# One decoder layer on one core: the second norm applied by VectorE, the tile turned in TensorE's transpose mode

## The chip, the core and the metric
The kernel runs on one core of one Trainium2 chip. The metric is the device time of one execution in microseconds (us), here the median of a few runs. A core has five engines that work side by side, each on its own queue in order: TensorE (PE) multiplies matrices and writes to PSUM, VectorE (DVE) and ScalarE (ACT) do elementwise work on SBUF and PSUM, GpSimd (POOL) builds a few constant masks, and SyncE (SP) issues the DMAs.

## What is computed
One layer of a decoder, on 1024 positions of 1024 channels, all float32. The mixer is a multi-scale causal pooling; a gated feed-forward network with a causal convolution follows.

```python
def rms_norm(x, g):
    return x * rsqrt(mean(x * x, axis=-1) + EPS) * g

h = rms_norm(x, norm_mix_g)
# four groups of 256 channels, windows of 2, 4, 8 and 16 positions:
d = causal_window_mean(h) - h
x = x + pool_scale * (einsum('bsgc,gcd->bsgd', d, pool_w) + pool_b)
n = rms_norm(x, norm_ffn_g)                    # the second norm
val, gate = split(causal_conv3(n @ w_in) + b)  # 2 x 2816 channels
x = x + (silu(gate) * val) @ w_out
```

## The kernel before, in words
A tile is 128 positions by 1024 channels, positions on the partitions; there are eight. The work has three parts: the mixer with the second norm (lines 384 to 413), the product with `w_in` for 22 pairs of hidden tiles (lines 263 to 447), and the product with `w_out` (lines 451 to 602). Both large products run as seven products of half-sized blocks (P1 to P7) in place of eight, and each float32 operand is split into a high and a low part in float32r, so that one product becomes three passes on TensorE. ScalarE makes the high part and VectorE subtracts it to get the low part (`split`, lines 67 to 71; `split_n`, lines 257 to 260).

The mixer is a software pipeline. Step j of the loop at line 389 scales the window matrix of tile j by the first norm's factor (`mixer_norm`), forms the windows of tile j-1 on TensorE (`mixer_window`, tile psd, split into dh and dl), multiplies tile j-2 by the pooling weights and adds the residual (`mixer_out`, tile psy), and prepares tile j-4 for the feed-forward part (`ffn_operand`, tile pst). Tiles psd, psy, pst and the edges share three PSUM pairs of banks (`bank2`).

The change is about the second norm. In the kernel before, `mixer_out` (lines 217 to 222) stores the new x1, computes one factor per position from its squares (`rstd_of`), and multiplies a 128x128 identity by that factor: a diagonal. `ffn_operand` (lines 233 to 255) then multiplies each 128x128 block of x1 by the diagonal on TensorE. This turns the block (channels on the partitions) and scales it in one matmul. With the channels on the partitions, the norm's gain is one number per partition: ScalarE applies it to seven blocks as it copies them from PSUM to `n2f` (`ACT_GAIN`, lines 241 to 242), VectorE to the eighth (line 244). The splits and subtractions that feed P1 to P7 then read `n2f`. Tiles 0 to 3 are split into B11 and B21; tiles 4 to 7 are subtracted from them (`sub`, line 271).

The tile framework sets the order on each engine at build time: it goes through the program, issues what its own times say is ready, in program order where several are, and gives out buffers from each pool. Work on an engine then runs strictly in that order. `tc.issue_after` (lines 408 and 421) holds the first splits of `w_in` behind a tile's residual add. The splits of weights, and some x tiles before them, share seven buffers of 4 KB per partition (tag `hl`). Everything in the pool `pre` (constants, the middle x tiles, the window matrices) is given back at line 414, and the later operands T2, T3, B22 and T4 take that room.

Of the kernel before, what the change touches and what calls it, by code (L numbers as in the profile page):

```python
# [7 lines left out]
F32 = mybir.dt.float32  # L8
F32R = mybir.dt.float32r
BF16 = mybir.dt.bfloat16  # L10
AF = mybir.ActivationFunctionType
ALU = mybir.AluOpType
PSUM = bass.MemoryType.PSUM

P = 128
S = 1024
D = 1024
F = 2816
NS = S // P
NK = D // P  # L20
NF = F // P
NG = 4
# [6 lines left out]
GF = GM + NK  # L29
# [1 line left out]

FAC = P
B0 = FAC + 2 * NG * HALO
BD = B0 + NG * P

NOPS_A = 3
ACT_GAIN = 7

NH = 512
NP2 = NF // 2  # L40
# [3 lines left out]
def trunk_kernel(ctx: ExitStack, tc: tile.TileContext, x, consts, par, rows, pool_w, w_in, w_out, out):  # L44
    nc = tc.nc
# [5 lines left out]
    work = ctx.enter_context(tc.tile_pool(name="work", bufs=1))  # L51
# [3 lines left out]
    pp = pre.enter_context(tc.tile_pool(name="pre", bufs=1, side="right"))  # L55
# [18 lines left out]
    xs = {}  # L74

    def load_x(j):
        if j < 2 or j == NS - 1:
            xs[j] = work.tile([P, D], F32, tag="hl", name=f"x{j}", bufs=7)
        else:
            xs[j] = pp.tile([P, D], F32, tag="x", name=f"x{j}", bufs=5)  # L80
        nc.sync.dma_start(xs[j], x[j * P : (j + 1) * P, :])

    cst = pp.tile([P, BD], F32, tag="cst", name="cst")
# [20 lines left out]
    par_sb = const.tile([P, NPAR], F32, tag="par", name="par_sb")  # L104
# [6 lines left out]
    nc.sync.dma_start(par_sb, par)  # L111
    nc.sync.dma_start(scale_b, rows[:1, :].to_broadcast([P, D]))
    load_x(1)
    for g in range(0, NG, 2):
        nc.sync.dma_start(wp_raw[:, 2 * g : 2 * g + 4, :], pool_w[g : g + 2].rearrange("g (k p) d -> p (g k) d", p=P))
    load_x(2)
# [5 lines left out]
    nc.vector.memset(eps_t, EPS)  # L122
    ident = cst[:, :FAC]
    fac = cst[:, FAC:B0].rearrange("p (c t) -> p c t", t=HALO)
    band0 = cst[:, B0:].rearrange("p (g s) -> p g s", s=P)

    def rstd_of(src, name):
        junk = pp.tile([P, D], BF16, tag="junk", name=f"junk_{name}")
# [22 lines left out]
            nc.tensor.matmul(ps[:, c * P : (c + 1) * P], src[:, c * P : (c + 1) * P], weights[:, c // 2, :], start=True, stop=True)  # L151


    bias_hl = pp.tile([P, D], F32R, tag="bias_hl", name="bias_hl")
    mean_w = pp.tile([P, P], F32R, tag="mean_w", name="mean_w")

    def mixer_bias():
        nc.vector.memset(mean_w.bitcast(F32), 2.0 / P)
        nc.vector.tensor_tensor(bias_b, bias_b, scale_b, ALU.mult)
        nc.scalar.activation(bias_hl, bias_b, AF.Copy)  # L160
        low = slice(P // 2, P)
        nc.vector.tensor_tensor(bias_hl[low, :], bias_b[low, :], bias_hl[low, :].bitcast(F32), ALU.subtract)
# [20 lines left out]
                nc.scalar.activation(wph[:, cs, :], wp_raw[:, cs, :], AF.Copy)  # L183
                nc.vector.tensor_tensor(wpl[:, cs, :], wp_raw[:, cs, :], wph[:, cs, :].bitcast(F32), ALU.subtract)

    ds = {}

    def mixer_window(j):
        ps = bank2(f"psd{j}")
# [13 lines left out]
    n2s = {}  # L203
    x1_dram = dram.tile([S, D], F32, tag="x1_dram", name="x1_dram")

    def mixer_out(j):
        dh, dl = ds.pop(j)
        ps = bank2(f"psy{j}")
        for h in range(2):
            cols = slice(h * NH, (h + 1) * NH)  # L210
            for c in range(4 * h, 4 * h + 4):
                o = ps[:, c // 2 * GRP : (c // 2 + 1) * GRP]
                for i, (a, w) in enumerate(((dh, wph), (dh, wpl), (dl, wph))):
                    nc.tensor.matmul(o, a[:, c, :], w[:, c, :], start=c % 4 == 0 and i == 0, stop=False, skip_group_check=True)  # L214
            nc.tensor.matmul(ps[:, cols], mean_w, bias_hl[:, cols], start=False, stop=True, skip_group_check=True)
        x1 = xs.pop(j)
        marks[j] = nc.vector.tensor_tensor(x1, ps, x1, ALU.add).ins
        nc.sync.dma_start(x1_dram[j * P : (j + 1) * P, :], x1)
        r = rstd_of(x1, f"b{j}")
        diag = pp.tile([P, P], F32, tag="diag", name=f"diag{j}", bufs=2)  # L220
        nc.vector.tensor_scalar(diag, ident, r, None, op0=ALU.mult)
        n2s[j] = (x1, diag)

    n2f = n2_pool.tile([P, NK, S], F32, tag="n2f", name="n2f")
    nops = {}
# [5 lines left out]
        nops[b] = nop_tile(nop_a, b)  # L231

    def ffn_operand(j):
        x1, diag = n2s.pop(j)
        ps = bank2(f"pst{j}")
        for c in range(NK):
            nc.tensor.matmul(ps[:, c * P : (c + 1) * P], x1[:, c * P : (c + 1) * P], diag, start=True, stop=True)  # L237
        cols = slice(j * P, (j + 1) * P)
        ps3 = ps.rearrange("p (c s) -> p c s", c=NK)
        gain = par_sb[:, GF : GF + NK]  # L240
        for c in range(ACT_GAIN):
            nc.scalar.activation(n2f[:, c, cols], ps3[:, c, :], AF.Identity, scale=gain[:, c : c + 1])
        rest = slice(ACT_GAIN, NK)
        nc.vector.tensor_tensor(n2f[:, rest, cols], ps3[:, rest, :], gain[:, rest].unsqueeze(2).to_broadcast([P, NK - ACT_GAIN, P]), ALU.mult)
        lo, hi = slice(0, 4), slice(4, 8)
        if j < NS // 2:
            split_n(nops["B11"], n2f[:, lo, cols], cols)
            split_n(nops["B21"], n2f[:, hi, cols], cols)
            return
        cols0 = slice(cols.start - NH, cols.stop - NH)  # L250
        b11, b12, b21, b22 = n2f[:, lo, cols0], n2f[:, lo, cols], n2f[:, hi, cols0], n2f[:, hi, cols]
        sub(b11, b12, b11)
        split_n(nops["T1"], b11, cols0)
        sub(b12, b22, b12)
        sub(b21, b21, b22)

    def split_n(t, src, cols=slice(None), ks=slice(None)):
        h = t[:, 0, ks, cols]
        nc.scalar.activation(h, src, AF.Copy)
        nc.vector.tensor_tensor(t[:, 1, ks, cols], src, h.bitcast(F32), ALU.subtract)  # L260
# [9 lines left out]
    def sub(out, a, b):  # L270
        nc.vector.tensor_tensor(out, a, b, ALU.subtract)  # L271
# [117 lines left out]
    for j in range(NS + 4):  # L389
        if j < NS:  # L390
            mixer_norm(j)
        if j == 0:
            edge_norm()
            stat(1)
        if 0 <= j - 1 < NS:
            mixer_window(j - 1)
        if j == 1:
            mixer_edges()
            mixer_weights()
            mixer_bias()  # L400
        if 0 <= j - 2 < NS:
            mixer_out(j - 2)
        if 0 <= j - 4 < NS:
            ffn_operand(j - 4)
        if j in (4, 6):
            load_in(j // 2 - 2)
        if 5 <= j <= 8:
            with tc.issue_after(marks[j - 2]):
                prep_event(j - 5)
        if j in (8, 10, 11):  # L410
            event((8, 10, 11).index(j))
        stat(j + 2)
        stat(j + 1)
# [10 lines left out]
    lo, hi = slice(0, 4), slice(4, 8)  # L424
    halves = [slice(0, 2), slice(2, 4)]
    t1, t3, b22, t4 = n2f[:, lo, s0], n2f[:, lo, s1], n2f[:, hi, s1], n2f[:, hi, s0]
# [119 lines left out]
    for k in range(-SLOOK, len(oevents)):  # L546
        p, f = oevents[k + SLOOK] if k + SLOOK < len(oevents) else (None, 0)
# [11 lines left out]
        p, f = oevents[k]  # L559
# [45 lines left out]
def constants():  # L605

    import numpy as np

    r, t, h = np.arange(P)[:, None], np.arange(P), np.arange(HALO)
    blocks = [np.eye(P)]  # L610
    blocks += [np.tile(w / np.minimum(h + 1, w), (P, 2)) for w in WINDOWS]
    inside = [(r > t - w) & (r <= t) for w in WINDOWS]
    blocks += [(m - np.eye(P) * np.minimum(t + 1, w)) / w for m, w in zip(inside, WINDOWS)]
    return np.concatenate(blocks, axis=1).astype(np.float32)


# [32 lines left out]
```

## Time and profile before
| | |
|---|---|
| median of 3 runs | 721.17 us (720.72 to 721.32) |
| the profiled execution | 723.45 us |
| its span, first to last instruction | 721.7 us |
| mean granted TensorE clock | 0.995 |
| ScalarE, busy share of the span | 49% |
| HBM read, written | 63.34 MB, 19.92 MB |

In a row of the timeline stand the start, the busy time, the engine, the line and operation, output and inputs, shapes and the count; in brackets, how long the engine idled before and what released it. Consecutive operations on one engine overlap a little in these rows, so what an operation costs its engine is the distance from its start to the next start. In a row of a group stand, after the bar, the busy time and the mean of one in ns, then the idle time ahead. A float32 matmul shows as two starts. A stretch's row begins with its two ends and its length.

### The profile page before, as it was taken

The page shows a single profiled execution, that of the slowest core. Times are in us where ns is not written, and L with a number is a line of the kernel's source. Part 1 is how long each engine was busy: PE and PEld are TensorE (multiplying, and loading weights), DVE is VectorE, ACT ScalarE, POOL GpSimd, SP SyncE. Part 2 cuts the span into 40 slices and gives each one's busy share as a digit, 9 for nine tenths or more (in the row PEclk, how much of TensorE's full clock was granted, in tenths as well). Part 3 has the DMA queues.
Part 4 walks back from the last instruction along what each step waited for, and adds up shares of the span by engine and source line. Part 5 has one row for each costly group of instructions (what it writes and reads, how often), then busy time and mean ns, then how long its engine had stood idle before and what let it go on. Part 6 is the DMA issues. An engine that isn't in the chain of part 4 may idle for free.

```text
span 721.7 us, 8803 instructions
## 1 busy us (share of the span) xinstructions
PE 698.9 (97%) x3252; PEld 580.2 (80%) x3252; DVE 609.7 (84%) x941; ACT 352.3 (49%) x566; POOL 7.7 (1%) x33
## 2 busy tenths in 40 slices
PE   3799999999999999999999999999999999999997
PEld 3799977888888888888888888888888788888886
DVE  3788999999888898888888888877996998798994
ACT  4597746554444444444444444444553444344441
POOL 4000000000000000000000000000000000000000
PEclk9899999999999999999999999999999999999999
DMA  9722030222222222222122112227999910005241
GB/s 266 282 89 84 34 117 0 118 88 88 88 87 88 88 88 89 87 88 81 66 89 73 58 75 87 88 89 264 315 321 312 308 54 1 0 1 190 87 152 67
DMA packets 30881, 83.83 MB, mean 116 GB/s; under 512 B 3335, under 2 KB 4487, under 8 KB 28023
## 3 DMA queue, kind: packets, MB, share of 16 engines
q1 hardware_dynamic: 30839, 83.28, 32.8%
q8 instruction: 25, 0.41, 0.2%
q14 instruction: 17, 0.14, 0.1%
HBM read 63.34 MB, written 19.92 MB: 115 GB/s over the span
## 4 chain that ended last, share of the span: by engine, by line
PE 80%; DVE 11%; DMA 6%; issue 1%; SPq 1%; ACT 1%; DVEq 0%; ACTq 0%
PE Y L303 23%; PE oP L576 21%; PE X L303 15%; PE Z L303 15%; PE psy L214 3%; DMA blk<-g_dram 3%; PE psd L151 2%; DMA x<-in_x_dram 1%; PE pst L237 1%; DVE n2f L271 1%; DVE oBP L70 1%; DVE T L260 1%; DMA blk<-in_w_out_dram 1%; DVE blk L271 1%; DVE oAP L70 1%
## 5 line engine op out<-in xcount | busy, mean ns | idle before, releaser
L576 PE MATMUL oP<-oBP,oAP 128*128 128x512 f32 x924 | 210.8, 390 | 1.0 <-ACT oBP L69 0.6
L576 PEld LDWEIGHTS oP<-oBP,oAP 128*128 128x128 f32 x924 | 173.2, 188 | 38.5 <-DVE oBP L70 1.4
L303 PE MATMUL X<-B,A11s 128*128 128x512 f32 x264 | 65.6, 394 | 0.7 <-DVE A11s L70 0.7
L303 PE MATMUL Y<-T,S2s 128*128 128x512 f32 x264 | 65.1, 394 | 1.1 <-DVE T L260 1.0
L303 PE MATMUL Z<-B,S4s 128*128 128x512 f32 x264 | 64.1, 392 | 0.6 <-DVE r L337 0.6
L303 PE MATMUL Z<-T,S1s 128*128 128x512 f32 x264 | 64.6, 393 | 0.0
L303 PE MATMUL Y<-T,S3s 128*128 128x512 f32 x264 | 64.3, 392 | 0.0
L303 PE MATMUL Y<-T,A22s 128*128 128x512 f32 x264 | 64.1, 392 | 0.0
L303 PE MATMUL X<-B,A12s 128*128 128x512 f32 x264 | 63.4, 390 | 0.0
L303 PEld LDWEIGHTS Y<-T,S2s 128*128 128x128 f32 x264 | 49.2, 188 | 13.2 <-DVE T L260 1.5
L303 PEld LDWEIGHTS X<-B,A11s 128*128 128x128 f32 x264 | 49.3, 188 | 12.3 <-DVE A11s L70 1.1
L303 PEld LDWEIGHTS Z<-B,S4s 128*128 128x128 f32 x264 | 49.5, 188 | 11.8 <-issue 1.1
L303 PEld LDWEIGHTS Z<-T,S1s 128*128 128x128 f32 x264 | 49.5, 188 | 11.4 <-ACT S1s L69 0.2
L303 PEld LDWEIGHTS Y<-T,S3s 128*128 128x128 f32 x264 | 49.6, 188 | 11.2
L303 PEld LDWEIGHTS Y<-T,A22s 128*128 128x128 f32 x264 | 49.5, 188 | 11.1 <-ACT val L350 0.3
L303 PEld LDWEIGHTS X<-B,A12s 128*128 128x128 f32 x264 | 49.5, 188 | 10.3
L361 ACT ACTIVATE gate<-gate 128x1024 f32<-128x1024 f32 x22 | 23.4, 1061 | 43.5 <-DVE gate L352 43.5
L69 ACT ACTIVATE oBP<-blk 128x512 fp32r<-128x512 f32 x32 | 20.2, 633 | 46.9 <-PE oP L576 41.6
L351 DVE SCALAR_TENSOR_TENSOR val<-ha,par_sb,val 128x1023 f32<-128x1023 f32 x22 | 28.2, 1282 | 12.5 <-ACT val L350 12.5
L343 DVE TENSOR_TENSOR ha<-Z,q 128x512 f32<-128x512 f32 x20 | 13.8, 691 | 23.9 <-PE Z L303 23.9
L69 ACT ACTIVATE S4s<-win 128x512 fp32r<-128x512 f32 x22 | 13.9, 633 | 40.4 <-PE Z L303 35.9
L350 ACT ACTIVATE gate<-hb,par_sb 128x1024 f32<-128x1024 f32 x22 | 27.4, 1245 | 11.9 <-DVE hb L345 11.9
(130 smaller groups left out, 1094.2 us busy)
## 6 DMA issues: line engine op xcount, KB each, us to landing
win<-in_w_in_dram SPq DMA_DIRECT2D x22, 1024.0 KB, 4.8
g_dram<-val SPq DMA_DIRECT2D x22, 512.0 KB, 2.6
blk<-g_dram SPq DMA_DIRECT2D x33, 256.0 KB, 5.4
blk<-in_w_out_dram SPq DMA_DIRECT2D x31, 256.0 KB, 5.5
A12s<-g_dram SPq DMA_DIRECT2D x22, 256.0 KB, 5.0
B21s<-in_w_out_dram SPq DMA_DIRECT2D x22, 256.0 KB, 3.5
x<-in_x_dram SPq DMA_DIRECT2D x8, 512.0 KB, 10.4
x_dram<-x SPq DMA_DIRECT2D x8, 512.0 KB, 2.6
```

The costliest lines, as they stand in the source:

```text
L69: nc.scalar.activation(t[:, 0, :], src, AF.Copy)
L70: nc.vector.tensor_tensor(t[:, 1, :], src, t[:, 0, :].bitcast(F32), ALU.subtract)
L151: nc.tensor.matmul(ps[:, c * P : (c + 1) * P], src[:, c * P : (c + 1) * P], weights[:, c // 2, :], start=True, stop=True)
L214: nc.tensor.matmul(o, a[:, c, :], w[:, c, :], start=c % 4 == 0 and i == 0, stop=False, skip_group_check=True)
L237: nc.tensor.matmul(ps[:, c * P : (c + 1) * P], x1[:, c * P : (c + 1) * P], diag, start=True, stop=True)
L271: nc.vector.tensor_tensor(out, a, b, ALU.subtract)
L303: nc.tensor.matmul(bank, a[:, i, ks], b[:, l, k, :], start=opens and m == 0, stop=m == 11, skip_group_check=not opens)
L343: tt(hid[n, "a"][:, NH:], bank, hid[n, "q2"], ALU.add)
L350: nc.scalar.activation(t, src, AF.Identity, bias=par_sb[:, CB + f : CB + f + 1], scale=w[2])
L351: nc.vector.scalar_tensor_tensor(t[:, 1:], src[:, : S - 1], w[1], t[:, 1:], op0=ALU.mult, op1=ALU.add)
L361: nc.scalar.activation(gate, gate, AF.Silu)
L576: nc.tensor.matmul(obanks[set_, i], a[:, u, i * P : (i + 1) * P], b[:, v, :], start=opens and g == 0 and m == 0, stop=g == NP2 - 1 and m = ...
```

## The change
The second norm is applied before the tile is turned. `mixer_out` makes `n2 = x1 * factor * gain` in one VectorE operation per tile, with the gain as a row repeated on all partitions. `ffn_operand` turns n2 with `nc.tensor.transpose`, and the splits and subtractions read the turned tile in PSUM where they can; ScalarE copies it to `n2f` without a scale (the whole tile for tiles 0 to 3, the upper half for tiles 4 to 7). The repeated row is made once by `gain_rows`: VectorE spreads the gain over an identity, TensorE sums over the partitions with two matmuls, ScalarE copies the result out of PSUM.

Four x tiles rather than three lie in the split weights' buffers at first (x0, x1, x6, x7), and so do the spread and the bias's two parts. x1 is no longer read by TensorE. The first tile's window matrix arrives packed as bf16, which makes the constants 256 KB rather than 384 KB.

```diff
-BD = B0 + NG * P
+BD = B0 + NG * P // 2
-ACT_GAIN = 7
+XBUFS = 4
...
-        if j < 2 or j == NS - 1:
+        if j < 2 or j >= 2 + XBUFS:
             xs[j] = work.tile([P, D], F32, tag="hl", name=f"x{j}", bufs=7)
         else:
-            xs[j] = pp.tile([P, D], F32, tag="x", name=f"x{j}", bufs=5)
+            xs[j] = pp.tile([P, D], F32, tag="x", name=f"x{j}", bufs=XBUFS)
...
     load_x(1)
+    spread = work.tile([P, NK, P], F32, tag="hl", name="spread", bufs=7)
+    bias_hl = work.tile([P, D], F32R, tag="hl", name="bias_hl", bufs=7)
...
-    band0 = cst[:, B0:].rearrange("p (g s) -> p g s", s=P)
+    band0 = cst[:, B0:].bitcast(BF16).rearrange("p (g s) -> p g s", s=P)
...
-    bias_hl = pp.tile([P, D], F32R, tag="bias_hl", name="bias_hl")
...
-    ds = {}
+
+    def gain_rows():
+        gain = par_sb[:, GF : GF + NK].unsqueeze(2).to_broadcast([P, NK, P])
+        nc.vector.tensor_tensor(spread, ident[:, None, :].to_broadcast([P, NK, P]), gain, ALU.mult)
+        ps = bank2("ps_gain")
+        flat = spread.rearrange("p k s -> p (k s)")
+        for h in range(2):
+            cols = slice(h * NH, (h + 1) * NH)
+            nc.tensor.matmul(ps[:, cols], mean_w.bitcast(F32), flat[:, cols], start=True, stop=True)
+        gain_b = work.tile([P, D], F32, tag="ha", name="gain_b", bufs=1)
+        nc.scalar.activation(gain_b, ps, AF.Copy, scale=P / 2.0)
+        return gain_b
+
+    ds, gains = {}, []
...
         r = rstd_of(x1, f"b{j}")
-        diag = pp.tile([P, P], F32, tag="diag", name=f"diag{j}", bufs=2)
-        nc.vector.tensor_scalar(diag, ident, r, None, op0=ALU.mult)
-        n2s[j] = (x1, diag)
+        n2 = n2s[j] = pp.tile([P, D], F32, tag="n2", name=f"n2_{j}", bufs=2)
+        nc.vector.scalar_tensor_tensor(n2, x1, r, gains[0], op0=ALU.mult, op1=ALU.mult)
...
     def ffn_operand(j):
-        x1, diag = n2s.pop(j)
+        n2 = n2s.pop(j)
         ps = bank2(f"pst{j}")
         for c in range(NK):
-            nc.tensor.matmul(ps[:, c * P : (c + 1) * P], x1[:, c * P : (c + 1) * P], diag, start=True, stop=True)
+            nc.tensor.transpose(ps[:, c * P : (c + 1) * P], n2[:, c * P : (c + 1) * P], ident)
         cols = slice(j * P, (j + 1) * P)
         ps3 = ps.rearrange("p (c s) -> p c s", c=NK)
-        gain = par_sb[:, GF : GF + NK]
-        for c in range(ACT_GAIN):
-            nc.scalar.activation(n2f[:, c, cols], ps3[:, c, :], AF.Identity, scale=gain[:, c : c + 1])
-        rest = slice(ACT_GAIN, NK)
-        nc.vector.tensor_tensor(n2f[:, rest, cols], ps3[:, rest, :], gain[:, rest].unsqueeze(2).to_broadcast([P, NK - ACT_GAIN, P]), ALU.mult)
         lo, hi = slice(0, 4), slice(4, 8)
         if j < NS // 2:
-            split_n(nops["B11"], n2f[:, lo, cols], cols)
-            split_n(nops["B21"], n2f[:, hi, cols], cols)
+            split_n(nops["B11"], ps3[:, lo, :], cols)
+            split_n(nops["B21"], ps3[:, hi, :], cols)
+            nc.scalar.activation(n2f[:, :, cols], ps3, AF.Copy)
             return
         cols0 = slice(cols.start - NH, cols.stop - NH)
-        b11, b12, b21, b22 = n2f[:, lo, cols0], n2f[:, lo, cols], n2f[:, hi, cols0], n2f[:, hi, cols]
+        b11, b12, b21, b22 = n2f[:, lo, cols0], ps3[:, lo, :], n2f[:, hi, cols0], n2f[:, hi, cols]
+        nc.scalar.activation(b22, ps3[:, hi, :], AF.Copy)
         sub(b11, b12, b11)
         split_n(nops["T1"], b11, cols0)
-        sub(b12, b22, b12)
+        sub(n2f[:, lo, cols], b22, b12)
         sub(b21, b21, b22)
...
             mixer_bias()
+            gains.append(gain_rows())
```

More of the change, by code (lines that the diff above doesn't have):

```diff
@@ L613, in constants @@
     blocks += [(m - np.eye(P) * np.minimum(t + 1, w)) / w for m, w in zip(inside, WINDOWS)]
-    return np.concatenate(blocks, axis=1).astype(np.float32)
+    blocks = [np.ascontiguousarray(b, dtype=np.float32) for b in blocks]
+    first = np.concatenate(blocks[1 + NG :], axis=1).view(np.uint32)
+    assert not (first & 0xFFFF).any()
+    packed = np.ascontiguousarray((first >> 16).astype(np.uint16)).view(np.float32)
+    return np.concatenate(blocks[: 1 + NG] + [packed], axis=1)
 def kernel(**inputs):
```

## The prediction
> **What bounds the kernel now.** I read the page's engine line first, then who waits for whom on TensorE, then busy time by stretch, then the order on TensorE and VectorE around the changed tiles.
>
> ```profile
> span 721.7 us, 8803 instructions
> PE 698.9 (97%) x3252; PEld 580.2 (80%) x3252; DVE 609.7 (84%) x941; ACT 352.3 (49%) x566; POOL 7.7 (1%) x33
> ```
> TensorE is busy for all but 22.8 us. By the engine shares alone, a change that shortens TensorE's work shortens the kernel. The waits say where that fails:
>
> ```profile
> PE psd L151 <- DVE bandr L147: 12.4, 3, 8.7
> PE Y L303 <- DVE T L260: 1.0, 1, 1.0
> PE X L303 <- DVE A11s L70: 0.7, 1, 0.7
> PE Z L303 <- DVE r L337: 0.6, 1, 0.6
> ```
> The first row is the start. The other three lie after the mixer, and all of them are waits for VectorE. The wait for A11s, the first operand of the third hidden tile, is the last of them (VectorE's row, then TensorE's):
>
> ```profile
> 111.15 0.68 DVE L70 TENSOR_TENSOR A11s<-win,A11s 128x512 fp32r<-128x512 f32 x1
> 111.88 2.56 PE L303 MATMUL X<-B,A11s 128*128 128x512 f32 x10 [0.70 <-DVE A11s L70]
> ```
> Busy time in the stretches up to and after that point (the columns are PE, PEld, DVE, ACT, POOL, granted clock, DMA share, GB/s):
>
> ```profile
> 30.19:40.03 9.84, 9.13 (x74) 8.77 (x73) 6.65 (x18) 7.45 (x15) 0.00 (x0) 1.00 0.44 177
> 40.03:75.55 35.52, 35.52 (x287) 34.57 (x286) 31.14 (x89) 28.40 (x74) 0.00 (x0) 1.00 0.19 75
> 75.55:111.88 36.33, 33.94 (x171) 27.84 (x169) 36.13 (x57) 23.27 (x48) 0.00 (x0) 1.00 0.20 73
> 111.88:150.00 38.12, 38.09 (x164) 30.40 (x165) 38.08 (x49) 21.37 (x28) 0.00 (x0) 1.00 0.14 56
> ```
> From 40.03 to 75.55 TensorE is the bound and VectorE idles 4.4 us of 35.5. From 75.55 to 111.88 VectorE is busy in 36.13 of 36.33 us and TensorE idles 2.4 us in three waits for it. After 111.88 TensorE hardly waits for anything until the end. So what counts is how late VectorE delivers A11s: that instant is 75.55 plus a stretch of VectorE without slack, and the rest of the kernel shifts with it. All eight changed tiles lie before it.
>
> **TensorE's part.** Four rows of its timeline make one step of the mixer:
>
> ```profile
> 46.93 1.95 PE L237 MATMUL pst<-diag,x 128*128 128x128 f32 x16
> 48.72 1.95 PE L151 MATMUL psd<-bandr,x 128*128 128x128 f32 x16
> 50.42 0.36 PE L214 MATMUL psy<-wph,dh 128*128 128x256 f32 x1
> 53.85 1.95 PE L237 MATMUL pst<-diag,x 128*128 128x128 f32 x16
> ```
> A step takes 6.92 us: 1.79 turning a tile, 1.70 windows, 3.43 mixer product. Turning a tile is 8 float32 matmuls that show as 16 starts, so in transpose mode it costs between nothing and 1.79 us. I take 0.9, eight single starts at the pace of this row. The step then needs 6.0 us of TensorE. Five tiles are turned ahead of 75.55, so TensorE alone would get there 4.5 us earlier, and all eight would give 7.1 us. The product on the mixer, the windows and the split products are untouched.
>
> **VectorE's part.** The rows that price it, from its timeline:
>
> ```profile
> 80.22 0.28 DVE L244 TENSOR_TENSOR n2f<-pst,par_sb 128x128 f32<-128x128 f32 x1
> 80.41 0.15 DVE L137 TENSOR_TENSOR st_b<-st_b 128x1 f32<-128x1 f32 x1
> 81.08 0.28 DVE L221 TENSOR_SCALAR diag<-cst,st_b 128x128 f32<-128x128 f32 x1
> 81.28 0.68 DVE L260 TENSOR_TENSOR T<-n2f,T 128x512 fp32r<-128x512 f32 x1
> 114.69 1.28 DVE L351 SCALAR_TENSOR_TENSOR val<-ha,par_sb,val 128x1023 f32<-128x1023 f32 x1
> 115.88 0.68 DVE L271 TENSOR_TENSOR win<-win 128x512 f32<-128x512 f32 x1
> ```
> By start to next start, the gain on the eighth block (L244) holds VectorE 0.19, say 0.20 us, the diagonal (L221) 0.20 us, and a scalar_tensor_tensor over 1023 columns from SBUF, the form of the new n2, 1.19 us. Each tile adds 1.19 and loses 0.20 for the diagonal: +0.99. It also loses 0.20 for L244, four steps of the loop after its mixer window. Eight tiles make 8 x 0.99 - 8 x 0.20 = +6.3 us on the engine that sets the instant of A11s.
>
> The splits and subtractions that now read PSUM keep their number: two per tile, 16 in all. Their price is read from two rows of the groups up to 112 us, one that reads PSUM (r from bank Z) and one that reads SBUF alone:
>
> ```profile
> L337 DVE TENSOR_TENSOR r<-Z,q 128x512 f32<-128x512 f32 x2 | 1.4, 680 | 0.0
> L70 DVE TENSOR_TENSOR A22s<-win,A22s 128x512 fp32r<-128x512 f32 x2 | 1.4, 680 | 0.0
> ```
> Both take 680 ns, so I count nothing for it. [...]
>
> **Where the +6.3 falls.** Ahead of 40.03 lies one n2 (tile 0), 0.99 us, where VectorE idles 9.84 - 6.65 = 3.2 us: nothing. In 40.03 to 75.55 lie six n2 and five removed L244: 6 x 0.99 - 5 x 0.20 = +4.9 us, against 4.4 us of idle time. These rows name that idle time (the waits from 36 to 75.55; columns are total, times, longest):
>
> ```profile
> DVE dl L200 <- PE psy L214: 3.7, 3, 2.2
> DVE n2f L271 <- ACT n2f L242: 1.0, 1, 1.0
> DVE psd L198 <- PE psd L151: 0.8, 1, 0.8
> DVE x L217 <- PE psy L215: 0.7, 1, 0.7
> ```
> Nearly all of it is waiting for TensorE, or for ScalarE's seven copies of a turned tile. Both get shorter, so most of it can be filled, but not all: the queue is in order, dl has one buffer and so waits for the whole mixer product before it. If everything is filled the stretch grows by 0.5, if nothing is, by 4.9. I take 1.4 us of idle time as left over, a third of the 4.4 and nearer the low end because the named causes shrink: +1.9. In 75.55 to 111.88 lie the last n2 and three removed L244: 0.99 - 0.60 = +0.4, without slack.
>
> **ScalarE.** Its rows for one tile:
>
> ```profile
> 47.09 1.05 ACT L199 ACTIVATE dh<-psd 128x1024 fp32r<-128x1024 f32 x1
> 49.88 1.65 ACT L242 ACTIVATE n2f<-pst,par_sb 128x128 f32<-128x128 f32 x6
> ```
> Seven scaled copies at 0.25 us become one copy over 1024 columns, 0.9 to 1.05 us, or a half of it in the second half of the tiles. The splits read PSUM at once and no longer wait for four copies. ScalarE is busy 28.40 of 35.52 us, so this buys latency, counted above, and no time of its own. The turned tile's PSUM pair is now held until VectorE's last subtraction from it; two other pairs remain, and by 75.55 only turned tiles need them: nothing.
>
> **The start.**
>
> ```profile
> 11.40:14.80 3.40, 1.04 (x8) 0.85 (x8) 1.45 (x7) 2.19 (x4) 0.00 (x0) 1.00 1.08 376
> 14.80:18.20 3.40, 2.97 (x15) 2.67 (x14) 2.63 (x9) 2.64 (x6) 0.00 (x0) 0.52 1.04 395
> 21.60:25.00 3.40, 0.94 (x6) 0.65 (x5) 3.40 (x11) 2.38 (x5) 0.00 (x0) 1.00 0.68 274
> 25.22:28.30 3.08, 3.08 (x13) 3.06 (x14) 2.21 (x6) 1.02 (x1) 0.00 (x0) 0.50 0.75 278
> 12.91 0.15 DVE L132 TENSOR_SCALAR st_e<-st_e 128x1 f32<-128x1 f32 x1 [4.31 <-ACT st_e L131]
> 22.84 1.21 DVE L159 TENSOR_TENSOR rows_b<-rows_b 128x1024 f32<-128x1024 f32 x1
> 23.97 0.68 DVE L184 TENSOR_TENSOR wpl<-wp_raw,wph 128x512 fp32r<-128x512 f32 x1
> 25.22 2.93 PE L151 MATMUL psd<-bandr,x 128*128 128x128 f32 x12 [2.66 <-DVE bandr L147]
> 27.81 0.77 PE L215 MATMUL psy<-bias_hl,mean_w 128*128 128x512 f32 x1
> ```
> The constants shrink by 128 KB ahead of the second x tile, at 376 to 395 GB/s 0.3 us: -0.3, since the DMA share is 1 there. The spread of the gain is one tensor_tensor over 1024 columns, 1.13 us by the row of rows_b. It needs only the constants and the parameters, so I expect it in the 4.31 us in which VectorE idles ahead of 12.91: 0, and +1.1 if it lands in the full stretch from 21.60 to 25.00. Its two matmuls cover 1024 columns as float32, as the turned tile does: 1.8 us at the same pace, in TensorE's idle time (2.4 us in 11.40 to 14.80, 2.5 in 21.60 to 25.00): 0. They could also hold the clock. After each of the two stretches with TensorE under a third busy, the granted clock is halved for the next; the twelve window matmuls at 25.22 then take 2.59 us where 16 take 1.70 at full clock, so holding it there is worth 2.59 - 1.28 = 1.3 us. I don't count it, because the matmuls are more likely to run in the first gap, which no one waits for. The gain's copy on ScalarE, about 1 us, falls where ScalarE is busy 2.38 of 3.40: nothing. The two tiles moved to the split weights' buffers (x6, x7), the bias halves and the spread leave four of seven buffers ahead of 75.55, and four splits are made by then: nothing.
>
> **The sum.** -0.3 + 0 + 1.9 + 0.4 = +2.0 us. The profiled execution took 723.45 us (span 721.7) and would take 725.45. The median of the runs is 721.17, 2.3 below it, and becomes 723.2.
>
> **Rivals.** Against a bound of 0.2% (1.4 us), about what a measurement here can tell from no change:
> - The two engines cancel: VectorE's idle time from 40.03 to 75.55 is filled to the last. -0.3 + 0.5 + 0.4 = +0.6, 721.8, no change. For it: TensorE runs a microsecond ahead in each step. Against: an in-order queue with single buffers. 0.32.
> - Faster, by the clock and a full VectorE: the gain's matmuls keep the clock up at 25.22 (-1.3) and VectorE also uses its idle time ahead of 40.03. It then does 37.79 + 5.9 us of work in the 45.36 from 30.19 to 75.55: -1.6. With -0.3 and +0.4 that is -2.8, 718.4. It decides only if VectorE idles under 2 us in that stretch, where it idles 7.6 now. 0.15.
> - None of the idle time is filled, and the spread sits in the full stretch: 4.9 + 0.4 - 0.3 + 1.1 = +6.1, 727.3. 0.08.
> [...]
> - Transpose mode is no shorter, 1.79 us a tile as now: the waits for TensorE stay and about 1.1 us of idle time is filled. 4.9 - 1.1 + 0.4 - 0.3 = +3.9, 725.1. 0.02.
>
> **How the numbers follow.** The forecast has 0.40. Faster 0.15, same 0.32, slower 0.40 + 0.08 + 0.03 + 0.02 = 0.53. The range from 719.0 to 726.8 leaves out most of the second rival and of the last microsecond of the third: under 2 in 10. The slower cases alone span 722.6 to 727.3.
>
> **What would show it.** In the profile after: pst under 1 us a tile on TensorE; n2 at 1.19 us a tile on VectorE; VectorE busy above 95% from 40 to 76; TensorE with new waits there for dl, bandr or n2; A11s of the third hidden tile about 2 us later than 111.2; TensorE's idle time up by some 7 us in all (7.1 saved, 1.8 added, 2.0 longer). The prediction is wrong if VectorE idles as much as before while TensorE waits (then the order is to blame), if the new work moves to a place where VectorE idled, or if A11s comes earlier than 111.

## The result and the profile after

| | before | after |
|---|---|---|
| median of 4 runs | 720.98 us (720.72 to 721.32) | 731.61 us (731.05 to 732.05) |
| the profiled execution | 723.45 us | 732.05 us |
| its span | 721.7 us | 730.3 us |

The kernel became slower: 1.014 times the time before, with a 95% interval of 1.0117 to 1.0162, about 10 us. The forecast was 2 us. The two profiled executions differ by 8.6 us, since the one of before lies 2.3 us above its own median and the one of after 0.4.

The engine line of the page of after answers to the one of before:

```profile
span 730.3 us, 8623 instructions
PE 698.2 (96%) x3192; PEld 575.1 (79%) x3192; DVE 615.9 (84%) x934; ACT 346.9 (48%) x519; POOL 7.7 (1%) x33
```
Eight turned tiles became shorter, and still TensorE is busy as long as before: 698.2 us against 698.9. TensorE at half clock counts as busy too (in before it is busy for all 3.08 us from 25.22, at a clock of 0.50), so this line doesn't say where the time is. The waits on TensorE do (in all, times, longest):

```profile
PE psd L155 <- DVE bandr L151: 8.7, 1, 8.7
PE ps_gain L197 <- DVE spread L192: 8.6, 1, 8.6
PE Z L315 <- ACT T L271: 1.9, 1, 1.9
PE psd L155 <- DVE dl L216: 1.8, 1, 1.8
PE psd L155 <- DVE x L233: 1.7, 3, 0.7
...
PE X L315 <- DVE A11s L72: 0.7, 1, 0.7
```
The first row is the start, as before. The second is new and the largest wait that before doesn't have. It is the one that the prediction had put at nothing: the gain's matmuls wait for the spread.

VectorE's timeline of after, from the edges to the first operand of the third hidden tile:

```profile
12.27 0.15 DVE L136 TENSOR_SCALAR st_e<-st_e 128x1 f32<-128x1 f32 x1 [3.65 <-ACT st_e L135]
...
24.46 0.47 DVE L151 TENSOR_SCALAR bandr<-band,st_a 128x512 f32<-128x512 f32 x1
24.84 1.22 DVE L192 TENSOR_TENSOR spread<-cst,par_sb 128x1024 f32<-128x1024 f32 x1
...
37.02 1.22 DVE L233 TENSOR_TENSOR x<-psy,x 128x1024 f32<-128x1024 f32 x1
...
81.76 1.23 DVE L233 TENSOR_TENSOR x<-psy,x 128x1024 f32<-128x1024 f32 x1
...
118.79 0.68 DVE L72 TENSOR_TENSOR A11s<-win,A11s 128x512 fp32r<-128x512 f32 x1
```
VectorE idles 3.65 us ahead of 12.27, and the spread is not there. It stands 12 us later, behind the third tile's window matrix (bandr at 24.46). TensorE's timeline of after at the same place:

```profile
13.78 3.78 PE L155 MATMUL ps_edges<-edge_band,x_edge 128*128 128x128 f32 x16 [1.33 <-DVE edge_band L147]
26.11 3.78 PE L197 MATMUL ps_gain<-spread,mean_w 128*128 128x512 f32 x4 [8.56 <-DVE spread L192]
29.69 3.00 PE L155 MATMUL psd<-bandr,x 128*128 128x128 f32 x16
32.45 0.36 PE L230 MATMUL psy<-wph,dh 128*128 128x256 f32 x1
```
Between the edges and the gain TensorE does nothing, and behind the gain come the windows of the second tile (psd) and the mixer's first product (psy). The same two in the timeline of before, and the residual adds of the first and the last tile:

```profile
18.81 2.05 PE L151 MATMUL psd<-bandr,x 128*128 128x128 f32 x16 [1.04 <-DVE bandr L147]
20.61 0.36 PE L214 MATMUL psy<-wph,dh 128*128 128x256 f32 x1
...
31.33 1.21 DVE L217 TENSOR_TENSOR x<-psy,x 128x1024 f32<-128x1024 f32 x1
...
75.75 1.23 DVE L217 TENSOR_TENSOR x<-psy,x 128x1024 f32<-128x1024 f32 x1 [0.42 <-PE psy L215]
```
The windows start 10.9 us later (18.81 to 29.69), and the first residual add 5.7 us later (31.33 to 37.02); the rest went into waits that before had at this place anyway, the 2.66 us for bandr among them. Three instants now divide the 8.6 us:

| | before | after | later by | of it new |
|---|---|---|---|---|
| first residual add (x of tile 0) | 31.33 | 37.02 | 5.69 | 5.69 |
| last residual add (x of tile 7) | 75.75 | 81.76 | 6.01 | 0.32 |
| A11s of the third hidden tile | 111.15 | 118.79 | 7.64 | 1.63 |
| end of the span | 721.7 | 730.3 | 8.6 | 1.0 |

Two thirds lie ahead of the first add. Busy time in stretches of after (PE, PEld, DVE, ACT, POOL, granted clock, DMA share, GB/s); the first answers to 21.60 to 25.00 before, the next two to 40.03 to 75.55 and 75.55 to 111.88, moved along by the delay:

```profile
21.60:25.00 3.40, 0.00 (x0) 0.00 (x0) 3.40 (x12) 2.19 (x5) 0.00 (x0) 0.51 0.58 233
45.72:81.56 35.84, 32.35 (x250) 30.23 (x249) 34.41 (x82) 25.66 (x46) 0.00 (x0) 1.00 0.19 74
81.56:119.53 37.97, 33.55 (x148) 26.03 (x146) 36.78 (x55) 20.10 (x30) 0.00 (x0) 0.96 0.18 70
91.60:95.00 3.40, 1.46 (x6) 0.66 (x4) 3.40 (x7) 2.84 (x5) 0.00 (x0) 1.00 0.02 5
95.00:98.40 3.40, 2.85 (x10) 2.29 (x10) 3.40 (x6) 1.21 (x2) 0.00 (x0) 0.76 0.00 0
```
In the mixer VectorE has become the engine that is nearly full: 34.41 of 35.84 us, against TensorE's 32.35. Behind the mixer TensorE waits for T (1.9 us in the table of waits); from 91.60 to 95.00 it is busy 1.46 of 3.40 us, and in the stretch after that the granted clock is 0.76, where before had 1.00.

### The profile page after: what moved, and what is told of

It reads as the page before. It is cut to its first block, busy times and chain, and to the rows that moved or that the text cites. A ratio compares the mean times of both kernels' runs of the same rounds, so it can differ in the third digit from the quotient of the medians.

```text
span 730.3 us, 8623 instructions
## 1 busy us (share of the span) xinstructions
PE 698.2 (96%) x3192; PEld 575.1 (79%) x3192; DVE 615.9 (84%) x934; ACT 346.9 (48%) x519; POOL 7.7 (1%) x33
## 4 chain that ended last, share of the span: by engine, by line
PE 76%; DVE 13%; DMA 8%; ACT 2%; issue 1%; SPq 1%; ACTq 0%; DVEq 0%
PE Y L315 22%; PE oP L589 21%; PE Z L315 15%; PE X L315 14%; DMA blk<-g_dram 3%; DMA blk<-in_w_out_dram 2%; DVE x L233 1%; DVE n2f L283 1%; DMA x_edge<-in_x_dram 1%; PE psy L230 1%; DVE T L272 1%; DVE n L237 1%; PE psd L155 1%; DMA B21s<-in_w_out_dram 1%; DMA A12s<-g_dram 1%
## 5 line engine op out<-in xcount | busy, mean ns | idle before, releaser
L315 PE MATMUL Z<-T,S1s 128*128 128x512 f32 x264 | 66.6, 401 | 2.5 <-ACT T L271 1.9
L341 ACT ACTIVATE ha<-X 128x512 f32<-128x512 f32 x22 | 13.2, 600 | 41.8 <-PE X L315 39.8
## 6 DMA issues: line engine op xcount, KB each, us to landing
x<-in_x_dram SPq DMA_DIRECT2D x8, 512.0 KB, 10.4
```

The lines of the kernel that those rows point to most:

```text
L315: nc.tensor.matmul(bank, a[:, i, ks], b[:, l, k, :], start=opens and m == 0, stop=m == 11, skip_group_check=not opens)
L341: nc.scalar.activation(hid[n, "a"][:, :NH], bank, AF.Copy)
```

## The experiments

The theory: the late spread, which holds back all that is queued behind the gain's matmuls on TensorE, makes most of the loss (START); VectorE's added work makes the rest (VECTOR). The rivals: TensorE's pace in the mixer decides, or the new PSUM and buffer holds do. Ratios are to the kernel before in the same session, with 95% intervals; instants are from each kernel's one profiled execution, and the first add varies from one execution to another by some 2 us (e9 shows it). The kernels were measured in three sessions, e1 to e4, e5 to e8 and e9 to e11, with 721.86 to 722.78 us as the median of before.

| | ratio | span | first add | last add | A11s |
|---|---|---|---|---|---|
| before | | 721.7 | 31.33 | 75.75 | 111.15 |
| after | 1.0140 (1.0117 to 1.0162) | 730.3 | 37.02 | 81.76 | 118.79 |
| e1 gain behind the first product | 1.0061 (1.0039 to 1.0084) | 725.9 | 32.09 | 78.38 | 114.44 |
| e2 before, with the gain's row | 1.0068 (1.0044 to 1.0092) | 725.9 | 36.10 | 80.89 | 116.29 |
| e3 gain by DMA | 1.0027 (1.0012 to 1.0042) | 724.3 | 31.58 | 76.02 | 112.40 |
| e4 e3, plain matmuls | 1.0061 (1.0044 to 1.0079) | 724.8 | 30.91 | 76.60 | 112.67 |
| e5 spread early | 1.0054 (1.0034 to 1.0075) | 722.4 | 31.98 | 76.30 | 112.08 |
| e6 e3, gain left out | 1.0006 (0.9992 to 1.0020) | 720.6 | 31.88 | 74.52 | 109.77 |
| e7 e3, n2 on ScalarE and GpSimd | 1.0156 (1.0139 to 1.0173) | 730.8 | 32.20 | 81.08 | 119.80 |
| e8 before, factor on ScalarE | 1.0029 (1.0012 to 1.0045) | 721.8 | 31.24 | 76.36 | 111.43 |
| e9 before, less on VectorE | 1.0010 (0.9991 to 1.0028) | 719.5 | 29.05 | 73.47 | 108.03 |
| e10 before, 20 more matmuls | 0.9999 (0.9987 to 1.0011) | 718.4 | 29.33 | 73.75 | 109.15 |
| e11 e9 and e10, packed constants | 0.9981 (0.9968 to 0.9994) | 719.5 | 30.04 | 74.45 | 109.00 |

From A11s to the end all of them take 609.3 to 612.1 us. So the instant of A11s decides a profiled span to within 1.5 us, as the prediction had it.

**e1: the gain's row made in `mixer_out`, behind the first tile's product.**

```diff
+        if not gains:
+            gains.append(gain_rows())
         n2 = n2s[j] = pp.tile([P, D], F32, tag="n2", name=f"n2_{j}", bufs=2)
...
             mixer_bias()
-            gains.append(gain_rows())
```


> The change, with one thing moved: the gain's spread and its two matmuls come in program order behind the first tile's mixer product, no longer ahead of the second tile's windows. Theory START: nearly all of the +10.6 us is lost before the first residual add (it starts at 37.02 us after the change, at 31.33 before), because TensorE's queue holds the second tile's windows behind the gain's matmuls, which wait for a spread that VectorE does at 24.84. Then the first residual add comes back to 31.5 to 32.5 and the time to 726.5 us (725.5 to 727.5). Rival LOAD: the extra 6.3 us of VectorE work in the mixer is what costs, and VectorE, full from there on, would have been late anyhow. Then the time stays at 730 or more.

The first add came at 32.09, 4.9 us earlier than in after, and the ratio fell from 1.0140 to 1.0061. Moving the same work in TensorE's order alone gives back more than half of the loss. It didn't give back all of the loss: the gain's first matmul now waited 4.8 us in the middle of the first product, and from the first add to A11s it takes 82.35 us, about as long as after (81.77) and 2.5 us longer than before.

**e2: before, with the gain's row made and used by nothing.** The spread lies in the split weights' buffers, as in after; all else is before.

```diff
+    spread = work.tile([P, NK, P], F32, tag="hl", name="spread", bufs=7)
...
             mixer_bias()
+            gains.append(gain_rows())
```


> The kernel before, with only the gain's repeated row added (spread, two matmuls, one copy, in the same place of the program); nothing reads it, the second norm is done as before. START: about +6 us, 727 (726 to 728): the same queue order, 0.3 us more than in the change since the constants are not packed. LOAD: 721 to 722.5, since only one VectorE operation is added.

Its timeline, TensorE's row and two of VectorE's:

```profile
25.14 1.21 DVE L191 TENSOR_TENSOR spread<-cst,par_sb 128x1024 f32<-128x1024 f32 x1
26.41 3.55 PE L196 MATMUL ps_gain<-spread,mean_w 128*128 128x512 f32 x4 [9.14 <-DVE spread L191]
...
36.10 1.21 DVE L230 TENSOR_TENSOR x<-psy,x 128x1024 f32<-128x1024 f32 x1
```
The same picture in a kernel that has nothing else of the change: the spread late, TensorE idle for 9.14 us ahead of it, the first add 4.8 us late, and 1.0068, or 4.9 us. These four instructions alone cost about half of what the whole change cost. About 6 us were expected, and the interval (3.2 to 6.6 us) holds them. START stands.

**e3: the repeated row read from memory by a broadcast DMA;** spread, matmuls and copy are gone, all else is as in after.

```diff
-        gain = par_sb[:, GF : GF + NK].unsqueeze(2).to_broadcast([P, NK, P])
...
-            gains.append(gain_rows())
+            gain_b = work.tile([P, D], F32, tag="ha", name="gain_b", bufs=1)
+            nc.sync.dma_start(gain_b, rows[2:, :].to_broadcast([P, D]))
+            gains.append(gain_b)
```


> The change, with the gain's row repeated over the partitions by a DMA behind the x tiles in place of spread, matmuls and copy. START: the first residual add at 30.7 to 31.3, and behind it what the change's profile shows behind that point (693.3 us to the end of the span, against 690.4 before): 723.3 us (722 to 724.5), +1 to +3.5 against before. LOAD: 729 or more.

1.0027, 1.9 us, the first add at 31.58. This is the change without its start, and the forecast for that part was +1.9 and +0.4. The trace puts it elsewhere than the forecast did: nothing between the first and the last residual add, 1.0 us from there to A11s. VectorE's column here is 34.05 us; the row stands beside the next two:

```profile
40.00:75.50 35.50, 32.55 (x250) 30.11 (x249) 34.05 (x84) 25.85 (x49) 0.00 (x0) 1.00 0.22 88
```

**e4: e3 with plain matmuls in place of the transposes.**

```diff
-            nc.tensor.transpose(ps[:, c * P : (c + 1) * P], n2[:, c * P : (c + 1) * P], ident)
+            nc.tensor.matmul(ps[:, c * P : (c + 1) * P], n2[:, c * P : (c + 1) * P], ident, start=True, stop=True)
```


> As the one with the gain by DMA, but the tile is turned by plain float32 matmuls with the identity (16 starts, 1.79 us a tile) in place of transpose mode (8 starts, 0.79 us by the change's timeline). If VectorE sets the pace of the mixer, as I said: 0 to 2 us above the run with transposes. If TensorE still sets it: 5 to 8 us above (8 x 1.0).

```profile
40.00:75.50 35.50, 34.91 (x278) 33.38 (x278) 34.38 (x84) 25.53 (x47) 0.00 (x0) 1.00 0.20 80
```
TensorE's column rises by 2.4 us, VectorE's stays. The plain matmuls cost 8.0 us more of TensorE over the eight tiles (8 x (1.79 - 0.79)), and of these 2.3 us arrive by the medians (727.58 and 725.27) and 0.5 by the spans; e4's profiled execution lies 1.0 us below its median and e3's 0.7 above. That is just above the 0 to 2 us expected if VectorE sets the pace, and well under the 5 to 8 us if TensorE does. So most of what transpose mode saves doesn't arrive: TensorE idles 2.95 us of the stretch in e3 and 0.59 in e4.

**e5: after with the spread early.** It takes another buffer and is held only behind the edges' norm; TensorE's order is that of after.

```diff
-    x_edge = work.tile([P, D], F32, tag="ha", name="x_edge", bufs=1)
+    x_edge = work.tile([P, D], F32, tag="hl", name="x_edge", bufs=7)
-    spread = work.tile([P, NK, P], F32, tag="hl", name="spread", bufs=7)
+    spread = work.tile([P, NK, P], F32, tag="ha", name="spread", bufs=1)
...
-        nc.vector.tensor_tensor(spread, ident[:, None, :].to_broadcast([P, NK, P]), gain, ALU.mult)
+        with tc.issue_after(marks["e"]):
+            nc.vector.tensor_tensor(spread, ident[:, None, :].to_broadcast([P, NK, P]), gain, ALU.mult)
```


> The change with its order on TensorE left as it is (gain's matmuls ahead of the second tile's windows), but the spread is made early on VectorE, right behind the edge window's factor at 13.2 to 13.7 us (it takes the one-buffer slot of the edge rows, which move to the seven buffers). If the start is lost to the wait of TensorE's queue for the spread: the first residual add at 31.5 to 32.5, the time 0.2 to 0.5% above the kernel before. If the two matmuls themselves cost it (their 3.6 us at half clock): the first residual add at 33 to 35 and 0.8% or more above.

Its timeline:

```profile
14.39 1.22 DVE L193 TENSOR_TENSOR spread<-cst,par_sb 128x1024 f32<-128x1024 f32 x1
...
16.41 1.88 PE L198 MATMUL ps_gain<-spread,mean_w 128*128 128x512 f32 x4
...
31.98 1.21 DVE L234 TENSOR_TENSOR x<-psy,x 128x1024 f32<-128x1024 f32 x1
...
112.08 0.67 DVE L72 TENSOR_TENSOR A11s<-win,A11s 128x512 fp32r<-128x512 f32 x1
```
Now it is what the prediction had drawn: the spread where VectorE idled, the gain's two matmuls at full clock in 1.88 us (1.8 was taken) in TensorE's gap, and the first add at 31.98. The ratio fell from 1.0140 to 1.0054. The place of one VectorE instruction of 1.2 us was worth about 6 us. Which of the two edits moved it, the buffer or the hold, isn't separated.

**e6: e3 with n2 = x1 x factor,** one tensor_scalar; it leaves the norm's gain out.

```diff
-        nc.vector.scalar_tensor_tensor(n2, x1, r, gains[0], op0=ALU.mult, op1=ALU.mult)
+        nc.vector.tensor_scalar(n2, x1, r, None, op0=ALU.mult)
```


> As the one with the gain by DMA, but n2 is x1 times the factor alone, a tensor_scalar of about 0.65 us in place of 1.19; the second norm's gain is left out of the computation. If VectorE's added work sets what is left of the loss (+1.9 us): 8 x 0.54 = 4.3 us less on VectorE, so 3 to 4.5 us below the one with the gain by DMA, a ratio of 0.996 to 0.999 to the kernel before. If the order or the buffers set it: within 1 us of the one with the gain by DMA.

```profile
40.00:75.50 35.50, 33.98 (x263) 31.51 (x262) 31.99 (x85) 26.42 (x48) 0.00 (x0) 1.00 0.22 85
```
The operation holds VectorE some 0.7 us rather than 1.2, VectorE's column falls from 34.05 to 31.99, TensorE's rises, and A11s comes 2.6 us earlier than in e3. The span falls by 3.7 us, as expected, but the ratio by 0.2%, 1.5 us, which is less than the 3 us expected; a likely reason is that TensorE, with VectorE lighter, is the fuller engine again. The difference from before can't be measured. Since e6 keeps the turned tiles in PSUM and the new buffers, little room is left for the rival that these holds make the loss.

**e7: e3 with the factor on ScalarE and the gain on GpSimd.**

```diff
-        nc.vector.scalar_tensor_tensor(n2, x1, r, gains[0], op0=ALU.mult, op1=ALU.mult)
+        nc.scalar.activation(n2, x1, AF.Copy, scale=r)
+        nc.gpsimd.tensor_tensor(n2, n2, gains[0], ALU.mult)
```


> As the one with the gain by DMA, but n2 leaves VectorE: ScalarE multiplies x1 by the factor (about 1.0 us), GpSimd by the row of gains; transpose mode stays. VectorE then has 8 x 0.40 = 3.2 us less than in the kernel before, TensorE 8 us less. If VectorE's load was the limit of transpose mode: 2 to 5 us below the kernel before (ratio 0.993 to 0.997). If GpSimd's multiply is long (over 4 us a tile) or slows VectorE: at or above the kernel before.

1.0156, the slowest of all, where 2 to 5 us below before was the better of the two expected outcomes. Its waits on TensorE:

```profile
PE pst L240 <- DVE x L220: 2.7, 1, 2.7
PE pst L240 <- POOL n L225: 2.5, 2, 1.6
PE psd L154 <- DVE x L220: 1.8, 1, 1.8
```
and its group on GpSimd:

```profile
L225 POOL TENSOR_TENSOR n<-n,gain_b 128x1024 f32<-128x1024 f32 x8 | 19.3, 2410 | 64.2 <-ACT n L224 64.2
```
GpSimd works 2.41 us a tile and waits 64.2 us for its input, so it isn't full. But it slows VectorE, which the other expected outcome had named:

```profile
45.93 2.39 POOL L225 TENSOR_TENSOR n<-n,gain_b 128x1024 f32<-128x1024 f32 x1 [5.24 <-ACT n L224]
46.33 2.01 DVE L138 SCALAR_TENSOR_TENSOR st_b<-st_b 128x1 f32<-128x1 f32 x1
49.11 1.22 DVE L220 TENSOR_TENSOR x<-psy,x 128x1024 f32<-128x1024 f32 x1
50.47 1.94 PE L240 MATMUL pst<-cst,n 128*128 128x128 f32 x8 [2.66 <-DVE x L220]
```
The small operation at 46.33, which takes 0.21 us elsewhere, lasts 2.01 and ends with GpSimd's multiply (48.34 and 48.32). The residual add behind it comes late, and the turn on TensorE waits for that add. During six of the eight multiplies one VectorE operation is held in this way; together these six last 10.4 us longer than their like. That is more than the 8 x 1.20 = 9.6 us of n2 that left VectorE. Of the three waits above, the first and the third are for residual adds behind held operations; only the second, 2.5 us, is for the longer way of n2 itself.

**e8: before with the factor applied to the tile on ScalarE and transpose mode;** the gain stays on the way out of PSUM, as before. Packed constants and buffers are as in after.

```diff
-        diag = pp.tile([P, P], F32, tag="diag", name=f"diag{j}", bufs=2)
-        nc.vector.tensor_scalar(diag, ident, r, None, op0=ALU.mult)
-        n2s[j] = (x1, diag)
+        n2 = n2s[j] = pp.tile([P, D], F32, tag="n2", name=f"n2_{j}", bufs=2)
+        nc.scalar.activation(n2, x1, AF.Copy, scale=r)
...
-            nc.tensor.matmul(ps[:, c * P : (c + 1) * P], x1[:, c * P : (c + 1) * P], diag, start=True, stop=True)
+            nc.tensor.transpose(ps[:, c * P : (c + 1) * P], n2[:, c * P : (c + 1) * P], ident)
```


> The kernel before with transpose mode alone: ScalarE multiplies x1 by the factor (1.0 us a tile), TensorE turns it in transpose mode, the gain is applied as before on the way out of PSUM (seven copies on ScalarE, one operation on VectorE); constants packed and buffers as in the change. VectorE loses 8 x 0.20 us, TensorE 8 x 1.0, ScalarE gains 8.0. If only VectorE limits: 1.5 to 4 us below the kernel before (0.994 to 0.998). If ScalarE, busy 28.4 of 35.5 us there, becomes the bound: 0 to 3 us above.

```profile
40.00:75.50 35.50, 31.63 (x243) 29.38 (x242) 29.74 (x83) 34.75 (x82) 0.00 (x0) 1.00 0.19 75
```
TensorE and VectorE both have room, and ScalarE is nearly full (34.75 of 35.50); VectorE waits 4.7 us for it in this stretch. The third engine now sets the pace, and the kernel is 0.3% slower than before. With e3 and e4 this speaks against TensorE's pace as the limit: in the mixer the three engines are so evenly loaded that work taken from one mostly returns on another.

**e9: before with less on VectorE.** The diagonal on ScalarE, all eight gains on ScalarE.

```diff
-ACT_GAIN = 7
+ACT_GAIN = 8
...
-        nc.vector.tensor_scalar(diag, ident, r, None, op0=ALU.mult)
+        nc.scalar.activation(diag, ident, AF.Copy, scale=r)
```


> The kernel before, with VectorE's two operations of the second norm's turn given to ScalarE (the diagonal, and the gain of the eighth block): VectorE 8 x 0.40 us lighter, ScalarE 8 x 0.5 us heavier. If the instant of A11s is set by VectorE alone from 75.55 on: one diagonal and three gains less in that stretch, 0.8 us earlier, a ratio of 0.998 to 1.000. If ScalarE already sets part of it: 1.000 to 1.003.

No difference that can be measured (1.0010), though from the first add to A11s it takes 78.98 us against 79.82, the 0.8 us that were expected. Its profile showed something else:

```profile
21.60:25.00 3.40, 2.00 (x12) 1.71 (x11) 3.37 (x11) 1.87 (x3) 0.00 (x0) 0.80 0.58 216
25.22:28.30 3.08, 3.08 (x26) 2.98 (x25) 1.90 (x6) 1.03 (x1) 0.00 (x0) 1.00 0.88 356
```
The first add came 2.3 us earlier than in before's profile, although up to it TensorE, VectorE and ScalarE run the same operations in the same order as there. So the start differs by this much from one execution to another, and the edit has no part in it. The clock goes with it: from 25.22 to 28.30 it is 1.00 here and 0.50 in before, but from 21.60 to 25.00 it is 0.80 here and 1.00 in before. e10 asked whether more work on TensorE ahead of 25 holds the clock up.

**e10: before with 20 more matmuls,** meant for TensorE's gap ahead of 25; nothing reads what they make. Fourteen of them run there, from 23.25 on; the others run earlier.

```diff
+            if j == 0 and h == 0:
+                warm = ps_x.tile([P, NH], F32, tag="X", name="warm")
+                for i in range(20):
+                    nc.tensor.matmul(warm[:, :GRP], dl[:, 0, :], wph[:, 0, :], start=True, stop=True)
```


> The kernel before, with 20 more matmuls on TensorE behind the first half of the first mixer product, into a PSUM bank that nothing reads; they change no output. If the halved clock from 25.2 to 28.3 us costs the start, as I priced it: the third tile's windows at full clock, the first residual add 1.0 to 1.5 us earlier, ratio 0.998. If the clock does not depend on the idle time ahead, or the time is lost elsewhere: 1.000 to 1.003.

```profile
21.60:25.00 3.40, 3.40 (x27) 3.40 (x27) 3.37 (x10) 1.88 (x3) 0.00 (x0) 0.88 0.70 233
25.22:28.30 3.08, 3.08 (x27) 3.00 (x27) 1.52 (x6) 1.03 (x1) 0.00 (x0) 1.00 0.90 354
```
In the profile the clock is 1.00 behind 25.22 and the first add 2.0 us earlier (29.33). But e9 shows the same without these matmuls, and here too the clock is lower in the stretch ahead: 0.88 in the first row, where the product's matmuls start 0.21 us apart from 21.76 to 22.40 and 0.12 apart from 22.66 on. So the profile doesn't show that they held the clock, and the ratio of 12 timed runs is 0.9999; the profiled execution is the shortest of the twelve (720.13 us, median 721.65).

The executions of before that were timed beside e1 to e11 point the same way. There are 64, from 719.49 to 725.39 us; the 30 with a mean granted clock of at most 0.995 have a median of 723.5 us, the 34 with at least 0.997 one of 721.8. The profiled one of before (723.45 us, 0.995) was among the longer. How much of its length is the clock at the start isn't separated.

**e11: e9, e10 and the packed constants together.**

```diff
-ACT_GAIN = 7
+ACT_GAIN = 8
...
+                warm = ps_x.tile([P, NH], F32, tag="X", name="warm")
...
+        nc.scalar.activation(diag, ident, AF.Copy, scale=r)
...
+    packed = np.ascontiguousarray((first >> 16).astype(np.uint16)).view(np.float32)
```


> The kernel before with both of these and with the constants packed as in the change (0.3 us): the sum of the parts, 2 us below the kernel before, ratio 0.996 to 0.998, if each of them lies on the way to A11s; 0.999 or more if they don't add up.

0.9981 (0.9968 to 0.9994): faster than before by 0.2%, 1.4 us, where 2 us were expected. Neither e9 nor e10 alone could be told from no change, and the packed constants weren't run alone, so which part does it stays open.

## Why the prediction was wrong

**The step that failed is "The start".** It read two right facts, VectorE's idle time ahead of 12.91 and TensorE's gaps, and concluded that the spread falls into the one and its matmuls into the other. Nothing in the page of before says so: the spread needs its inputs early, but where it stands in VectorE's order is set when the kernel is built, and it was set at 24.84. What put it there stays open: in e1 the program writes it later still, and it stands at 25.18 all the same. The worse error was the price of that case. The prediction named it, "+1.1 if it lands in the full stretch from 21.60 to 25.00", and counted only the spread's own 1.1 us on VectorE. It didn't ask what is queued behind the gain's matmuls on TensorE. That is the second tile's windows and the first mixer product, and they cost 5.69 us at the first add. The prediction gave that price to its third rival as well, which so stopped at 727.3. e2 shows the price by itself (4.9 us by the ratio), e5 shows that most of it goes when the spread is early.

A ledger from the ratios, each times 721 us: after is 10.1 us above before. The early spread takes 6.2 of it away (e5), no spread and matmuls at all 1.9 more (e3), a lighter n2 1.5 more (e6), and 0.4 is left, within what can be measured. Each of these differences crosses sessions and is uncertain by 1.5 to 2.2 us, worked out from the intervals of the two ratios, so the last two are barely clear of nothing. The start alone (e2, 4.9) and the rest alone (e3, 1.9) add up to 6.8 of the 10.1, and the 3.3 left over is a little more than the uncertainty of this comparison, 2.6. Of the 10.1 us about 2 are not in the difference of the two traces. Two reasons are on record, and how much each makes stays open: before's profiled execution was a long one (e9 reaches the first add 2.28 us earlier with the same order up to it), and before's median in the later sessions, 721.86 to 722.78 us, would put after only 8.8 to 9.8 us above it.

**The middle, 40.03 to 75.55, +1.9: too large.** Between the first and the last residual add after takes 0.32 us longer than before, e3 0.0 and e5 0.1 less. VectorE left 1.43 us of the stretch idle (35.84 - 34.41), and 1.4 was taken; but its column rose by 3.3 us there and not by the 4.9 that was counted (31.14 to 34.41), though the operations are the counted ones (six n2, none of the six diagonals and five gains). Where the other 1.6 us of counted work went wasn't settled.

**The last stretch, +0.4: measured +1.63.** VectorE's work grew by 0.65 us (36.13 to 36.78), near the forecast, and 1.0 us is new idle time: TensorE waited 1.9 us for T, its clock fell to 0.76 after that, and VectorE then waited 1.16 us for the bank Z. That the one brought on the other is read from their order in time, not from a run. Middle and last together were +2.3 and measured +1.95 in after, +1.0 in e3 and +0.3 in e5. The prediction's first rival, that the engines cancel, lies nearer to the last of these than the forecast does.

**The prices of single operations: right.** One turned tile, from its start to the next matmul's in TensorE's timeline of after:

```profile
74.60 1.04 PE L252 MATMUL pst<-cst,n 128*128 128x128 f32 x8
75.39 3.01 PE L315 MATMUL X<-B,A11s 128*128 128x512 f32 x12
```
0.79 us for 8 starts; 0.9 was taken, and 1.79 was the plain form. The rival that transposes are no shorter is out. One n2 and the operation behind it in VectorE's:

```profile
43.48 1.28 DVE L237 SCALAR_TENSOR_TENSOR n<-x,st_b,gain_b 128x1024 f32<-128x1024 f32 x1
44.68 0.21 DVE L139 SCALAR_TENSOR_TENSOR st_a<-st_a 128x1 f32<-128x1 f32 x1
```
1.20 us; 1.19 was taken. The reads from PSUM, by two groups of after from 40 to 120 us, one that reads PSUM and one that reads SBUF alone:

```profile
L272 DVE TENSOR_TENSOR B<-pst,B 128x512 fp32r<-128x512 f32 x8 | 5.5, 682 | 0.1
...
L272 DVE TENSOR_TENSOR T<-n2f,T 128x512 fp32r<-128x512 f32 x4 | 2.8, 689 | 0.0
```
No added cost: 682 ns with the read from PSUM, 689 without. The -0.3 for the packed constants isn't shown by any run: the edges' norm comes 0.64 us earlier in after (12.91 to 12.27), but over all profiles it comes at 11.73 to 13.02 with them and at 12.03 to 13.14 without.

**The clock in the mixer** stayed at 1.00 from 45.72 to 81.56 in after, with TensorE busy for 32.35 of 35.84 us. The 0.03 in the prediction's chances is for a drop of the clock there: neither profile shows one (1.00 from 40.03 to 75.55 in before). In e7, with TensorE busy for 29.37 of 35.50 us, the clock was 0.95 from 40.00 to 75.50.

**The signs that the prediction named.** A turned tile under 1 us (0.79), n2 at 1.20 us and a VectorE above 95% in the mixer (34.41 of 35.84) came in; A11s came 7.64 us later and not 2. Its first sign of being wrong, TensorE waiting while VectorE idles as before (then the order is to blame), came in too, but at the start and not in the mixer: TensorE waits 8.56 us for a spread that isn't in VectorE's 3.65 us of idle time. Three quarters of A11s's 7.64 us came from the start and not, as forecast, from the mixer.

## What to carry to other kernels

An added operation costs what it does itself, and also what stands behind it in the in-order queue of the engine that waits for it: before calling a small operation free, name its neighbours in both queues, and price the case in which its operand comes last. A gap in a trace is no promise that the new work will be placed there; where the place matters, it has to be fixed in the order. And where three engines share a stage at 80 to 100% each, moving work between them returns a fraction (in e4 0.5 to 2.3 of 8 us), so the likeliest outcome of such a move is none; in e7, where the work went to GpSimd, it was a loss (1.0156).

## What the runs showed of the hardware

- The granted clock fell after stretches in which TensorE was busy for a part of the time. In after, a stretch with 1.46 of 3.40 us busy (43%), at 1.00 itself, is followed by one at 0.76; in before, 0.94 of 3.40 (28%), at 1.00, by one at 0.50. Whether a share of busy time decides it can't be read from such cuts: e9's stretch with 2.00 of 3.40 busy (59%) is followed by 1.00, but has 0.80 itself.
- The gain's two float32 matmuls took 1.88 us at a clock of 1.00 (e5) and 3.55 and 3.78 at 0.50, where TensorE had idled for 9.14 us (e2) and 8.56 us (after) before them: what had waited long also took twice as long.
- On 128x1024 float32, a multiply of two tensors took 2.41 us on GpSimd (e7), where VectorE does it in 1.2 (the spread) and ScalarE scales a tile in 1.2 (e8). While it ran, six VectorE operations that read only SBUF took longer (the one at 46.33 took 2.01 us rather than 0.21 and ended with it). The residual add at 75.10, which reads PSUM, was not held (1.21 us, with GpSimd busy from 74.25 to 76.66), and neither were two small ones that read SBUF (46.07 and 46.14, 0.15 us each, with GpSimd busy from 45.93 to 48.32).
